# Two tiles' q and k turned into one bank ahead of its copies

## The chip, the cores and the metric

The kernel runs on one core of a Trainium2 chip. The metric is the device time of one execution in microseconds. Before the change three runs took 1618.83, 1619.05 and 1622.59 us; their median is 1619.05 us. Less is better.

## The reference

One layer of a bidirectional encoder: a sequence of 1024 tokens, model width 1024, everything in float32. Two attention branches share one input projection, and a gated feed-forward block follows. What concerns the change is the normalised q and k of each attention head:

```python
proj = h @ w_in[l]
qa, ka, va, qb, kb, vb, gates = jnp.split(proj, split_at, axis=-1)

qa = rms_norm(qa.reshape(b, s, NA_HEADS, HEAD_DIM), g_qa[l])
ka = rms_norm(ka.reshape(b, s, NA_HEADS, HEAD_DIM), g_ka[l])
o_a = neighbourhood_attention(qa, ka, va, rpb[l])

qb = partial_rotary(rms_norm(qb.reshape(b, s, DIL_HEADS, HEAD_DIM), g_qb[l]), pos)
kb = partial_rotary(rms_norm(kb.reshape(b, s, DIL_HEADS, HEAD_DIM), g_kb[l]), pos)
for g, (win, dil) in enumerate(DIL_CONFIGS):
    o_g, lse_g = dilated_window_attention(qb[:, :, sl], kb[:, :, sl], vb[:, :, sl], win, dil)
```

There are 12 dilated heads in three groups (windows 128, 512 and 2048 with dilations 1, 4 and 16) and 8 neighbourhood heads, each of 64 columns. The scores multiply q with k over these 64 columns, so both are needed with the columns on the partitions, that is, transposed.

## The kernel before, in words

The heads are worked on in pairs, called units: two units for each of the three dilated groups (kinds 0, 1 and 2, units 0 to 5) and four for neighbourhood attention (kind 3, units 6 to 9). A unit has 8 tiles of 128 tokens. One counter n runs over the tiles, u, t = divmod(n, 8), and iteration n projects tile t of unit u: 8 chunks (proj_chunk, L288) of three matmuls of 384 columns (high part times high part, high times low, low times high) into a bank of tag "d", four chunks in the first half of the iteration, four in the second. After that proj_post (L305) reads the bank: ScalarE squares and copies q and k (sq, qn), VectorE sums and scales (L314 to L316), GpSimd does the rotary part of kinds 0 to 2 (L323 to L326). The tile qn then holds the finished q (columns 0 to 127) and k (128 to 255), tokens on the partitions.

qk_turn (L347) turns a tile: two TensorE transposes of 128 x 128 (L352) into PSUM, and four copies out of it. ScalarE writes the high part of q with its gain (L370) and the high part of k (L371); VectorE writes the remainders of both (L372, L373). The parts go to U.qk, in an order of tokens that depends on the unit's kind. Each of these four copies has 128 columns.

Up to n = 57 the attention work stands in the middle of every odd iteration, between the two halves of the projection: scores of a cluster of items (L511), its maxima on VectorE (L521) and exponentials on ScalarE (L523), the product with v of the cluster from two odd iterations before (L556), the turns of two tiles (those of iterations n - 3 and n - 2), and the transposes of the previous cluster's P (L536). Such a pair of turns shares one PSUM bank of 512 columns: the first tile takes columns 0 to 255, the second 256 to 511. Unit 0 has four pairs (n = 8, 9, 11 and 13), the later units 24. From n = 58 on each iteration turns one tile alone, in a bank of its own; there are 24 of these.

A bank (L68) is a PSUM tile of one tag out of "d", "s", "v" and "t", two buffers each. Dependencies are kept for the tile: a write into a bank waits for the reads of it that stand earlier in the program. TensorE's order is the order of the program. In this part of the kernel the order on ScalarE, VectorE, GpSimd and the DMA queue is set by a scheduler that plays a timeline, with a priority on some functions. The weights of the next unit are loaded during a unit and split into a high part (ScalarE, L108) and a low part (GpSimd or VectorE, L109) at its end, six of the eight in t = 7, into ten buffers of each kind.

Beside this VectorE sums a vector-matrix product from loads of wa (L282), with a row sum on TensorE every eight steps (L259), and prepares pieces for later stages (L719 to L729).

Of the kernel before, what the change touches and what calls it, by code (L numbers as in the profile page):

```python
# [42 lines left out]
def hybrid_layer(ctx: ExitStack, tc: tile.TileContext, x, colp, wada1, wada2, bada2, wqkv, wg, wpa, wpb,  # L43
                 wo, w1, w2, hgain, ropeg, rope, rbias, bmask, g2r, out):
    nc = tc.nc
# [22 lines left out]
    def bank(tag):  # L68
        return ps.tile([128, 512], F32, tag=tag, name="ps_" + tag)
# [9 lines left out]
    ident = const.tile([128, 128], F32, name="ident")  # L79
# [16 lines left out]
    def fview(ap):  # L96
        return ap.bitcast(F32)
# [6 lines left out]
    def wsplit(r, eng=None):  # L104
        n = r.shape[1]
        hi = wp.tile([128, 512], F32R, tag="hi", bufs=NHL, name="whi")
        lo = wp.tile([128, 512], F32R, tag="lo", bufs=NHL, name="wlo")
        nc.scalar.activation(hi[:, :n], r, AF.Copy)  # L108
        (eng or nc.gpsimd).tensor_sub(lo[:, :n], r, fview(hi[:, :n]))  # L109
        return hi, lo  # L110
# [56 lines left out]
    def unit_load(u, k):  # L167
        return wload(wqkv[u, :, k, :], 384)
# [119 lines left out]
    def proj_chunk(U, t, k):  # L288
        if k == 0:
            U.pd[t] = bank("d" if U.u else "t")  # L290
        pd = U.pd[t]
        for i, (a, b) in enumerate(PASS):
            nc.tensor.matmul(pd[:, :384], tok(a, k, t), U.w[k][b][:, :384],  # L293
                             start=(k == 0 and i == 0), stop=(k == KT - 1 and i == 2))

    def urgent(off):
        def deco(f):
            def g(*a):
                with tc.high_priority(off):
                    return f(*a)  # L300
            return g
        return deco
# [41 lines left out]
                    nc.sync.dma_start(U.v[:, j, :], vv[j])  # L344

    @urgent(QT)
    def qk_turn(U, t, tag="v", pt=None):  # L347
        qf = U.qn[t].rearrange("p h d -> p (h d)")
        if pt is None:
            pt = bank(tag)  # L350
        for i in range(2):
            nc.tensor.transpose(pt[:, i * 128:(i + 1) * 128], qf[:, i * 128:(i + 1) * 128], ident)  # L352
        g = hg[:, 0:1] if U.kind == 3 else hg[:, 2:3]
        ops = []
        for i in range(2):
            hi, lo = U.qk[2 * i], U.qk[2 * i + 1]
            src = pt[:, i * 128:(i + 1) * 128]
            if U.kind == 0:
                hi, lo = hi[:, t * 128:(t + 1) * 128], lo[:, t * 128:(t + 1) * 128]
            elif U.kind < 3:  # L360
                n = 4 * U.kind
                c = slice(t * 128 // n, (t + 1) * 128 // n)
                hi, lo = (z.rearrange("p (r i) -> p r i", r=n)[:, :, c] for z in (hi, lo))
                src = src.rearrange("p (i r) -> p r i", r=n)
            else:
                hi, lo = (z.rearrange("p (w r) -> p r w", r=16)[:, 2 * t:2 * t + 2] for z in (hi, lo))
                src = src.rearrange("p (r w) -> p r w", r=2)
            ops.append((hi, lo, src))
        (qh, ql, qs), (kh, kl, ks) = ops
        nc.scalar.activation(qh, qs, AF.Identity, scale=g)  # L370
        nc.scalar.activation(kh, ks, AF.Copy)  # L371
        nc.vector.scalar_tensor_tensor(ql, qs, g, fview(qh), op0=ALU.mult, op1=ALU.subtract)  # L372
        nc.vector.tensor_sub(kl, ks, fview(kh))  # L373

    def new_unit(u, w):
        U = Unit()
        U.kind, U.pair = UNITS[u]
        U.u = u
        U.w = w
        U.pd, U.qn = {}, {}  # L380
        qk = ap_.tile([128, 4, S], F32R, tag="qk", bufs=2, name="qk")
        U.qk = [qk[:, i, :] for i in range(4)]
        U.v = big("v", [128, 8, 128])
        if U.kind < 3:
            U.tab = rtab[0] if rtab else None
            U.st = ap_.tile([128, 9, 4], F32, tag="st", bufs=2, name="st")
        else:
            U.bias = []
            for h in range(2):
                b = big("rb", [128, 768])  # L390
                nc.sync.dma_start(b, rbias[U.pair * 2 + h])
                U.bias.append(b)
        return U
# [352 lines left out]
    U = new_unit(0, w0)  # L746
# [143 lines left out]
    for n in range(6, 92):  # L890
        u, t = divmod(n, 8)
        if u < 10:
            if t == 0:
                units.append(new_unit(u, [nextw[u, k] for k in range(KT)]))
            U = units[u]
            chunks = [lambda k=k, U=U, t=t: proj_chunk(U, t, k) for k in range(KT)]
        elif n - 80 < NPRE:
            chunks = gate_pre(n - 80)
        else:
            chunks = []  # L900
        if u + 1 < 10:
            for k in ([0, 1, 2, 3, 4, 5, 6, 7] if n == 6 else [t] if u else []):
                raws[u + 1, k] = unit_load(u + 1, k)
            if t == 6:
                for k in range(2):
                    nextw[u + 1, k] = wsplit(raws[u + 1, k])
        if t == 2 and 1 <= u <= 10:
            for slot, I in unit_items(units[u - 1]):
                if I.U.kind < 3:
                    waiting.append(I)  # L910
                else:
                    ready.setdefault(8 * u + 2 + slot, []).append(I)
        if n == 8 * 7 + 5:
            combine_stats()
        ci = n - (8 * 7 + 7)
        if 0 <= ci < 12:
            combine_prep(ci)
        if n >= PAIRED:
            done, prev, cur = prev, cur, ready.pop(n, [])
        elif n % 2:  # L920
            done, prev, cur = prev, cur, []
            if waiting:
                cur = [Cluster()]
                while waiting and cur[0].keys + waiting[0].nkb * 128 <= 512:
                    cur[0].add(waiting.pop(0))
        else:
            done = []

        def chunk():
            if chunks:  # L930
                chunks.pop(0)()
                k = 8 - len(chunks)
                if t == 7 and u + 1 < 10 and k < 8 and k >= 2:
                    nextw[u + 1, k] = wsplit(raws[u + 1, k], nc.vector if k % 2 else None)

        turns = [(units[0], tt) for tt in {8: (0, 1), 9: (2, 3), 11: (4, 5), 13: (6, 7)}.get(n, ())]
        if PAIRED <= n <= 81 or 9 < n < PAIRED and n % 2:
            turns += [(units[m // 8], m % 8) for m in ((n - 2,) if n >= PAIRED else (n - 3, n - 2)) if m >= 8]
        chunk()
        chunk()  # L940
        chunk()
        chunk()
        if n < 10:
            while chunks:
                chunk()
        if n >= PAIRED or n % 2 or n < 10:
            for I in cur:
                if I.__class__ is Cluster:
                    cl_scores(I)
                    cl_qk(I)  # L950
                else:
                    at_scores(I)
                    at_qk(I, 0)
                    at_qk(I, 1)
            for I in done:
                (cl_pv if I.__class__ is Cluster else at_pv)(I)
            for j, q in enumerate(turns):
                if j % 2 == 0:
                    pq = bank("s" if n < 10 else "v")
                qk_turn(*q, "v", pq[:, 256 * (j % 2):256 * (j % 2) + 256])  # L960
            for I in prev:
                if I.__class__ is Cluster:
                    cl_turn(I)
                else:
                    at_turn(I, 0)
                    at_turn(I, 1)
        chunk()
        chunk()
        chunk()
        chunk()  # L970
        if n >= 8 and (t != 7 or u > 8) and ada_state["i"] < 65:
            ada_step()
        if 2 <= u < 6 and t < 5:
            if t in (2, 4):
                t_piece(2 * (u - 2) + t // 2 - 1, 2)
            if t in (0, 2):
                t_piece(2 * (u - 2) + t // 2, 0)
            if t in (1, 3):
                t_piece(2 * (u - 2) + t // 2, 1)
        if n in (85, 88):  # L980
            w1_combos((n - 85) // 3, EARLY[(n - 85) // 3])
        if 1 <= ci < 13:
            combine_step(ci - 1)
        while chunks:
            chunk()
        if u < 10:
            proj_post(U, t)
# [642 lines left out]
```

## Time and profile before

| what | value |
|---|---|
| median of 3 runs | 1619.05 us |
| profiled execution | 1627.35 us |
| its span, first to last instruction | 1625.5 us |
| mean granted TensorE clock over the span | 0.971 |
| TensorE busy | 1538.7 us, 95% |
| VectorE busy | 1109.7 us, 68% |
| ScalarE busy | 670.8 us, 41% |
| GpSimd busy | 532.2 us, 33% |

The engines are called PE (TensorE's matmuls), PEld (its weight loads), DVE (VectorE), ACT (ScalarE), POOL (GpSimd) and SP (the queue of loads and stores). A row of a timeline gives start and duration in us, engine, line, and what is written from what; in brackets the idle time before it on its engine and what ended that time. A list of waits gives the waiting line, the line waited for, the total in us, the number of times and the longest. Where a wait has several conditions, the row names what came last by the profile, which need not be the condition that mattered. The windows view cuts the span into stretches and gives busy times and the clock that TensorE was granted, 1.00 being full speed.

### The profile page before, as it was taken

Reading aid. Unit: us, or ns where it says so; the run is one execution under the profiler, and the core shown is the slowest. Engines: PE = TensorE matmul, PEld = TensorE weight load, DVE = VectorE, ACT = ScalarE, POOL = GpSimd, SP = SyncE. Lnnn points to the kernel's source line nnn. Section 1 sums busy time; section 2 is a strip of 40 time slices with the busy share of each in tenths; the row PEclk is TensorE's granted clock in tenths of the full one; section 3 lists DMA queues with packets and bytes.
Section 4 is the critical chain, followed back from the end, with each engine's and each line's share of the span. In section 5 each row is a group of like instructions: output and inputs, shape, how many; then the busy total and the mean of one; then the engine's idle time right before and its main releaser. Section 6 shows DMA issues by size and latency. Waiting matters only on the chain. (4 is left out here: it accounts for less than half of the span.)

```text
span 1625.5 us, 24441 instructions
## 1 busy us (share of the span) xinstructions
PE 1538.7 (95%) x8156; PEld 1301.9 (80%) x8156; DVE 1109.7 (68%) x2374; ACT 670.8 (41%) x1694; POOL 532.2 (33%) x540
## 2 busy tenths in 40 slices
PE   9978788888889999999999999999999999999998
PEld 7877778777778878788887888888888888887887
DVE  6745565555568996446567449778877777589567
ACT  5535444444445445433454234433223333344442
POOL 0512122122011001300045221167767777302564
PEclk9989898998999999999999999999999999999999
DMA  9603353343243343565354523534543333699343
GB/s 367 220 9 111 120 161 95 114 155 95 69 153 103 113 149 91 179 194 222 101 160 137 186 82 102 178 119 145 179 143 104 104 104 112 204 365 338 109 151 101
DMA packets 154414, 241.66 MB, mean 149 GB/s; under 512 B 26656, under 2 KB 73376, under 8 KB 153520
## 3 DMA queue, kind: packets, MB, share of 16 engines
q1 hardware_dynamic: 153136, 235.90, 44.5%
q10 hardware_dynamic: 1152, 4.19, 0.7%
q8 instruction: 65, 1.06, 0.3%
q14 instruction: 61, 0.50, 0.1%
HBM read 179.89 MB, written 60.15 MB: 148 GB/s over the span
## 5 line engine op out<-in xcount | busy, mean ns | idle before, releaser
L109 POOL TENSOR_TENSOR wlo<-raw,whi 128x512 fp32r<-128x512 f32 (+2 forms) x133 | 174.3, 1320 | 501.7 <-ACT whi L108 316.8
L293 PE MATMUL ps_d<-whi,hT 128*128 128x384 f32 x1152 | 329.9, 359 | 0.0
L108 ACT ACTIVATE whi<-raw 128x512 fp32r<-128x512 f32 (+1 forms) x348 | 205.5, 600 | 291.8 <-PE ps_s L1466 36.1
L109 DVE TENSOR_TENSOR wlo<-raw,whi 128x512 fp32r<-128x512 f32 (+1 forms) x215 | 181.6, 857 | 80.4 <-ACT whi L108 76.5
L293 PEld LDWEIGHTS ps_d<-whi,hT 128*128 128x128 f32 x1152 | 227.3, 203 | 5.2 <-issue 2.6
L293 PE MATMUL ps_d<-wlo,hT 128*128 128x384 f32 x576 | 203.7, 354 | 0.4 <-POOL wlo L109 0.4
L293 PEld LDWEIGHTS ps_d<-wlo,hT 128*128 128x128 f32 x576 | 117.0, 203 | 0.7 <-POOL wlo L109 0.7
L352 PE MATMUL ps_v<-ident,qn 128*128 128x128 f32 x152 | 35.0, 317 | 66.9 <-DVE qk L373 53.6
L108 ACT ACTIVATE whi<-ws 128x512 fp32r<-128x512 f32 x65 | 40.9, 629 | 130.1 <-DVE ws L1313 76.3
L323 POOL TENSOR_TENSOR ra<-qn,rtab 128x64 f32<-128x64 f32 x48 | 16.3, 339 | 231.4 <-DVE qn L316 212.7
L1246 POOL TENSOR_TENSOR e<-e,c 128x512 f32<-128x512 f32 x44 | 68.5, 1557 | 63.9 <-DVE c L1376 39.7
L314 DVE TENSOR_REDUCE ss<-sq 128x4 f32<-128x256 f32 x80 | 33.3, 416 | 74.2 <-ACT sq L311 74.1
L352 PEld LDWEIGHTS ps_v<-ident,qn 128*128 128x128 f32 x152 | 16.3, 150 | 80.5 <-issue 42.3
L311 ACT ACTIVATE sq<-ps_d 128x256 f32<-128x256 f32 x74 | 28.2, 382 | 112.7 <-PE ps_d L293 109.7
L109 POOL TENSOR_TENSOR wlo<-m,whi 128x512 fp32r<-128x512 f32 x35 | 51.6, 1483 | 54.4 <-ACT whi L108 54.4
L523 ACT ACTIVATE P<-P,st 128x256 f32<-128x256 f32 (+2 forms) x100 | 45.3, 455 | 41.8 <-DVE st L521 41.8
L680 PE MATMUL ps_d<-hT,whi 128*128 128x512 f32 x192 | 60.6, 396 | 0.0
L1296 PE MATMUL ps_v<-h2T,whi 128*128 128x512 f32 x192 | 59.3, 390 | 0.0
L1296 PE MATMUL ps_s<-h2T,whi 128*128 128x512 f32 x192 | 59.2, 390 | 0.0
L459 ACT ACTIVATE P<-P,sx 128x384 f32<-128x384 f32 (+1 forms) x64 | 37.0, 579 | 50.5 <-DVE sx L458 50.5
L1244 ACT ACTIVATE e<-e 128x512 f32<-128x512 f32 x44 | 27.4, 630 | 72.5 <-DVE e L1379 47.2
L1296 PE MATMUL ps_d<-h2T,whi 128*128 128x512 f32 x184 | 56.9, 390 | 0.0
(445 smaller groups left out, 4057.2 us busy)
## 6 DMA issues: line engine op xcount, KB each, us to landing
raw<-in_w_dram SPq DMA_DIRECT2D x139, 256.0 KB
ga_d<-e SPq DMA_DIRECT2D x77, 256.0 KB
raw<-ga_d SPq DMA_DIRECT2D x77, 256.0 KB
wa<-in_wada_dram SPq DMA_DIRECT2D x32, 512.0 KB
raw<-in_wqkv_dram SPq DMA_DIRECT2D x80, 192.0 KB
m<-in_w_dram SPq DMA_DIRECT2D x44, 256.0 KB
raw<-in_wg_dram SPq DMA_DIRECT2D x42, 256.0 KB
xt<-in_x_dram SPq DMA_DIRECT2D x16, 512.0 KB
```

The lines of the kernel that those rows point to most:

```text
L108: nc.scalar.activation(hi[:, :n], r, AF.Copy)
L109: (eng or nc.gpsimd).tensor_sub(lo[:, :n], r, fview(hi[:, :n]))
L293: nc.tensor.matmul(pd[:, :384], tok(a, k, t), U.w[k][b][:, :384], start=(k == 0 and i == 0), stop=(k == KT - 1 and i == 2))
L311: nc.scalar.activation(sq, pd[:, :256], AF.Square)
L314: nc.vector.tensor_reduce(ss, sq.rearrange("p (h d) -> p h d", h=4), axis=mybir.AxisListType.X, op=ALU.add)
L352: nc.tensor.transpose(pt[:, i * 128:(i + 1) * 128], qf[:, i * 128:(i + 1) * 128], ident)
L459: nc.scalar.activation(P[:nq, :nk], P[:nq, :nk], AF.Exp, scale=-1.0, bias=nm, accum_out=sm)
L523: nc.scalar.activation(C.P[h][:nq, c], C.P[h][:nq, c], AF.Exp, scale=-1.0, bias=nm, accum_out=sm)
L680: nc.tensor.matmul(st["p"], gw[i, br][j][a][:, kk * 128:(kk + 1) * 128], hT[b][:, k, hs], start=(k == 0 and q == 0), stop=(k == 7 and q == 2))
L1244: nc.scalar.activation(sg, a, AF.Sigmoid)
L1246: nc.gpsimd.tensor_mul(sg, sg, up)
L1296: nc.tensor.matmul(pb, w[p][:, k * 128:(k + 1) * 128], b[q][:, k], start=(k == 0 and i == 0), stop=(k == 3 and i == 2))
```

## The change

The turn of two tiles becomes one function, qk_turns. It issues all four transposes into one bank, sorted q of the first tile, q of the second, k of the first, k of the second, and then copies out with four instructions of 256 columns (qk_parts) in place of eight of 128. The two tiles are neighbours, so their tokens lie side by side in each of the layouts. A single tile goes through the same functions with n = 1: as before, two transposes and four copies of 128 columns.

```diff
     @urgent(QT)
-    def qk_turn(U, t, tag="v", pt=None):
-        qf = U.qn[t].rearrange("p h d -> p (h d)")
-        if pt is None:
-            pt = bank(tag)
-        for i in range(2):
-            nc.tensor.transpose(pt[:, i * 128:(i + 1) * 128], qf[:, i * 128:(i + 1) * 128], ident)
+    def qk_turns(tiles, tag):
+
+        bk = bank(tag)
+        n = len(tiles)
+        for j, (U, t) in enumerate(tiles):
+            qf = U.qn[t].rearrange("p h d -> p (h d)")
+            for i in range(2):
+                c = (i * n + j) * 128
+                nc.tensor.transpose(bk[:, c:c + 128], qf[:, i * 128:(i + 1) * 128], ident)
+        qk_parts(*tiles[0], n, bk)
+
+    def qk_parts(U, t, n, bk):
+
         g = hg[:, 0:1] if U.kind == 3 else hg[:, 2:3]
         ops = []
         for i in range(2):
             hi, lo = U.qk[2 * i], U.qk[2 * i + 1]
-            src = pt[:, i * 128:(i + 1) * 128]
+            src = bk[:, i * n * 128:(i + 1) * n * 128]
             if U.kind == 0:
-                hi, lo = hi[:, t * 128:(t + 1) * 128], lo[:, t * 128:(t + 1) * 128]
+                hi, lo = (z[:, t * 128:(t + n) * 128] for z in (hi, lo))
             elif U.kind < 3:
-                n = 4 * U.kind
-                c = slice(t * 128 // n, (t + 1) * 128 // n)
-                hi, lo = (z.rearrange("p (r i) -> p r i", r=n)[:, :, c] for z in (hi, lo))
-                src = src.rearrange("p (i r) -> p r i", r=n)
+                m = 4 * U.kind
+                c = slice(t * 128 // m, (t + n) * 128 // m)
+                hi, lo = (z.rearrange("p (r i) -> p r i", r=m)[:, :, c] for z in (hi, lo))
+                src = src.rearrange("p (i r) -> p r i", r=m)
             else:
-                hi, lo = (z.rearrange("p (w r) -> p r w", r=16)[:, 2 * t:2 * t + 2] for z in (hi, lo))
-                src = src.rearrange("p (r w) -> p r w", r=2)
+                hi, lo = (z.rearrange("p (w r) -> p r w", r=16)[:, 2 * t:2 * t + 2 * n] for z in (hi, lo))
+                src = src.rearrange("p (r w) -> p r w", r=2 * n)
             ops.append((hi, lo, src))
         (qh, ql, qs), (kh, kl, ks) = ops
         nc.scalar.activation(qh, qs, AF.Identity, scale=g)
...
-            for j, q in enumerate(turns):
-                if j % 2 == 0:
-                    pq = bank("s" if n < 10 else "v")
-                qk_turn(*q, "v", pq[:, 256 * (j % 2):256 * (j % 2) + 256])
+            for j in range(0, len(turns), 2):
+                qk_turns(turns[j:j + 2], "s" if n < 10 else "v")
```

In the changed kernel the transposes stand in L355, the copies in L377 to L380, and the lines behind them are numbered 7 higher (5 higher from L964 on).

TensorE at the first pair, n = 8 (qn is the tile that is turned, ps_s the bank; brackets name what a row waits for), before and then after:

```order
L293 MATMUL ps_d<-whi,hT_391 128x384
L352 MATMUL ps_s<-ident,qn 128x128 [waits PE_49]
L352 MATMUL ps_s<-ident,qn 128x128
L352 MATMUL ps_s<-ident,qn 128x128 [waits DVE_49]
L352 MATMUL ps_s<-ident,qn 128x128
L293 MATMUL ps_d<-whi,hT_106 128x384
```

```order
L293 MATMUL ps_d<-whi,hT_391 128x384
L355 MATMUL ps_s<-ident,qn 128x128 [waits PE_49]
L355 MATMUL ps_s<-ident,qn 128x128 x3
L293 MATMUL ps_d<-whi,hT_106 128x384
L293 MATMUL ps_d<-wlo,hT_106 128x384
```

The wait for VectorE between the two tiles is gone; the number and place of the transposes are the same.

TensorE at the pair of n = 15 (tiles 12 and 13; the pair that the prediction shows in the timeline), before and then after:

```order
L556 MATMUL ps_v<-PT,v 64x128 x2
L352 MATMUL ps_v<-ident,qn 128x128 [waits Pool_49]
L352 MATMUL ps_v<-ident,qn 128x128
L352 MATMUL ps_v<-ident,qn 128x128 [waits DVE_49,Pool_49]
L352 MATMUL ps_v<-ident,qn 128x128
L536 MATMUL ps_t<-ident,P 128x128 x8
```

```order
L563 MATMUL ps_v<-PT,v 64x128 x4
L355 MATMUL ps_v<-ident,qn 128x128 [waits DVE_49,Pool_49]
L355 MATMUL ps_v<-ident,qn 128x128
L355 MATMUL ps_v<-ident,qn 128x128 [waits DVE_49,Pool_49]
L355 MATMUL ps_v<-ident,qn 128x128
L543 MATMUL ps_t<-ident,P 128x128 x8
```

The rows stand in the same order. The second tile's wait still names both engines, which both write qn; the first tile's now names VectorE too, and the rows before it have fewer waits.

ScalarE at the same pair, before and then after:

```order
L523 ACTIVATE P,st<-P,st 128x256 [waits DVE_49] x2
L370 ACTIVATE qk<-ps_v,hg 128x128 [waits PE_49]
L371 ACTIVATE qk<-ps_v 128x128
L523 ACTIVATE P,st<-P,st 128x256 [waits DVE_49] x2
L370 ACTIVATE qk<-ps_v,hg 128x128 [waits DVE_49,PE_49]
L371 ACTIVATE qk<-ps_v 128x128
L545 ACTIVATE PT<-ps_t 128x512 [waits PE_49]
```

```order
L530 ACTIVATE P,st<-P,st 128x256 [waits DVE_49] x2
L377 ACTIVATE qk<-ps_v,hg 128x256 [waits PE_49]
L378 ACTIVATE qk<-ps_v 128x256
L530 ACTIVATE P,st<-P,st 128x256 [waits DVE_49] x2
L552 ACTIVATE PT<-ps_t 128x512 [waits PE_49]
```

The copies of both tiles now stand where the first tile's stood, in the middle of the exponentials; the second pair of copies is gone.

## The prediction

> **What bounds the kernel now.** I read the page first, then one stretch of the windows view, then TensorE's own waits in that stretch, then the timeline around one pair of turns. The page says where TensorE's time is not at full clock (forty slices of 40.6 us):
>
> ```profile
> span 1625.5 us, 24441 instructions
> ...
> PEclk9989898998999999999999999999999999999999
> ```
>
> The low digits stand in the first twelve slices, so in the projection stage. The windows view of that stage (n = 8 to 57, 73 to 474 us), of four short stretches inside it, and of the stretch just after it; columns: stretch, length, busy us of PE, PEld, DVE, ACT and POOL with instruction counts, granted clock, DMA share, GB/s:
>
> ```profile
> 73.00:474.00 401.00, 329.62 (x2088) 303.58 (x2087) 226.98 (x776) 179.66 (x645) 81.46 (x204) 0.89 0.35 108
> 127.00:131.00 4.00, 1.14 (x16) 0.72 (x14) 3.91 (x16) 2.15 (x9) 1.44 (x4) 0.85 0.73 207
> 131.00:134.00 3.00, 2.91 (x13) 2.94 (x14) 1.05 (x3) 1.47 (x5) 0.33 (x2) 0.50 0.61 238
> 134.00:137.00 3.00, 3.00 (x12) 3.00 (x11) 0.74 (x2) 1.57 (x3) 1.03 (x2) 0.56 0.00 0
> 137.00:140.00 3.00, 3.00 (x19) 3.00 (x18) 1.70 (x6) 1.63 (x6) 2.00 (x2) 1.00 0.01 3
> 474.00:570.00 96.00, 93.50 (x671) 82.37 (x671) 85.09 (x287) 50.96 (x172) 7.75 (x7) 1.00 0.39 119
> ```
>
> TensorE idles 401.00 - 329.62 = 71.4 us of the stage and has a mean clock of 0.89; after it, where turns come singly, it is 97% busy at 1.00. DVE is at 57% in the stage and ACT at 45%: neither bounds it. TensorE's waits in 73 to 474 us, the whole list (total us, times, longest):
>
> ```profile
> PE ps_v L352 <- DVE qk L373: 53.6, 21, 6.2
> PE ps_v L352 <- POOL rb L325: 8.8, 3, 3.0
> PE ps_v L352 <- POOL qn L326: 4.6, 2, 2.6
> PE ps_s L352 <- DVE qk L373: 4.5, 2, 2.6
> ```
>
> They sum to 71.5 us in 28 waits, as many as there are pairs of turns (4 of unit 0, 24 of later units), and all stand before one line, the transposes of qk_turn. So the idle time of the stage is this one wait. The timeline of one pair (start, us, engine, line) shows what it is:
>
> ```profile
> 127.70 0.44 PE L352 MATMUL ps_v<-ident,qn 128*128 128x128 f32 x2
> ...
> 129.85 0.34 ACT L370 ACTIVATE qk<-ps_v,hg 128x128 fp32r<-128x128 f32 x1
> 130.11 0.26 ACT L371 ACTIVATE qk<-ps_v 128x128 fp32r<-128x128 f32 x1
> 130.39 0.35 DVE L372 SCALAR_TENSOR_TENSOR qk<-ps_v,hg,qk 128x128 fp32r<-128x128 f32 x1
> 130.66 0.28 DVE L373 TENSOR_TENSOR qk<-ps_v,qk 128x128 fp32r<-128x128 f32 x1
> 131.09 0.66 PE L352 MATMUL ps_v<-ident,qn 128*128 128x128 f32 x2 [2.95 <-POOL rb L325]
> 131.54 1.91 PE L536 MATMUL ps_t<-ident,P 128*128 128x128 f32 x8
> ...
> 133.58 0.52 PE L293 MATMUL ps_d<-wlo,hT 128*128 128x384 f32 x1
> 134.54 0.52 PE L293 MATMUL ps_d<-wlo,hT 128*128 128x384 f32 x1
> ...
> 137.07 0.33 PE L293 MATMUL ps_d<-wlo,hT 128*128 128x384 f32 x1
> 137.59 0.33 PE L293 MATMUL ps_d<-wlo,hT 128*128 128x384 f32 x1
> ```
>
> Tile 12's q and k are transposed at 127.70. Tile 13's go into the same bank and stand still until the last of tile 12's four copies has left it (L373 ends at 130.94). The row names POOL only because a rotary step happened to end then too; the copy is what the bank waits for. ACT and DVE get to these copies late, because the exponentials and maxima of the cluster stand ahead of them. After the wait the clock is half: chunks of three matmuls follow each other at 134.54 - 133.58 = 0.96 us, against 137.59 - 137.07 = 0.52 us once it is back, and the windows show 0.50 and 0.56 there.
>
> **The change, part by part.**
>
> *1. The wait goes.* All four transposes stand ahead of any copy, and the order shows that the second tile's lose their DVE wait at n = 8 and keep elsewhere only waits for their own inputs. 28 waits, 71.4 us. Those inputs must be there earlier now. The latest case of the stage:
>
> ```profile
> 175.89 0.44 PE L352 MATMUL ps_v<-ident,qn 128*128 128x128 f32 x2
> 176.00 0.38 POOL L326 TENSOR_TENSOR qn<-ra,rb 128x64 f32<-128x64 f32 x1
> ```
>
> Tile 19's last rotary step ends at 176.38, while its transposes could now start at 175.89 + 0.44 = 176.33; by the same rows of the other 27 pairs (L326, or L316 where a unit has no rotary) the input was there before the first tile's transposes began, in two of them by under 0.35 us. Between the end of a projection and its turn lie an even iteration, half an odd one and the attention matmuls, all PE work and no pair wait, so this margin shrinks only where the clock was low there.
>
> *2. The half clock goes with it.* Two estimates. The first: 0.11 of 401 us is 44 us of lost clock. Part of it fell into the waits themselves, where it costs nothing (0.15 x 4 = 0.6 us in 127 to 131); at 0.4 a pair that is 11 us, and 33 us stay. The second compares periods:
>
> ```profile
> 147.43 0.41 PE L352 MATMUL ps_v<-ident,qn 128*128 128x128 f32 x2 [1.83 <-DVE qk L373]
> ...
> 199.76 0.41 PE L352 MATMUL ps_v<-ident,qn 128*128 128x128 f32 x2 [2.86 <-POOL rb L325]
> 200.00 1.04 PE L536 MATMUL ps_t<-ident,P 128*128 128x128 f32 x8
> ...
> 211.25 0.44 PE L352 MATMUL ps_v<-ident,qn 128*128 128x128 f32 x2
> ...
> 470.39 0.44 PE L352 MATMUL ps_v<-ident,qn 128*128 128x128 f32 x2 [1.52 <-DVE qk L373]
> ```
>
> From second turn to second turn 20 periods take (470.39 - 147.43) / 20 = 16.15 us. The stretch 199.76 to 211.25, 11.49 us, ran at full clock (its eight transposes took 1.04 us, against 1.91 at 131.54). A mean period without its wait (71.4 / 28 = 2.55) and the first turn (0.44) is 13.16, 1.67 above it. Some of it is work that only a few periods have, the one-row sums:
>
> ```profile
> L259 PE MATMUL ps_t<-acc,ones 128*1 128x512 f32 x10 | 5.1, 591 | 0.0
> ```
>
> Over 24 periods that is 0.2, so 1.47 a pair, 41 us over 28. I take 35, nearer to the first estimate, which counts the whole stage and not one stretch as the yardstick.
>
> *3. Fewer, wider copies.* Per pair eight copies become four of 256 columns. Price, from the forms view (mean ns of one):
>
> ```profile
> L370 ACT ACTIVATE qk<-ps_v,hg 128x128 fp32r<-128x128 f32 x52 | 19.5, 375 | 34.1 <-PE ps_v L352 34.1
> L372 DVE SCALAR_TENSOR_TENSOR qk<-ps_v,hg,qk 128x128 fp32r<-128x128 f32 x52 | 18.8, 362 | 35.1 <-ACT qk L371 34.8
> ...
> L311 ACT ACTIVATE sq<-ps_d 128x256 f32<-128x256 f32 x50 | 19.1, 382 | 98.2 <-PE ps_d L293 98.1
> L564 DVE COPY stg<-ps_v 128x256 f32<-128x256 f32 x15 | 6.2, 416 | 0.0
> ```
>
> A 256-column read of PSUM takes 0.38 on ACT and 0.42 on DVE, against 0.36 and 0.36 for 128 columns with the gain. At 0.4 to 0.5 each, a pair costs ACT 0.9 instead of 1.2 us, DVE 0.9 instead of 1.3. Neither bounds the stage, so I count nothing; at worst, were they as dear as two narrow ones, still nothing changes. The copies as a whole start about 0.5 us later for the first tile; their readers are the scores two iterations on.
>
> *4. What becomes late next.* PE now reaches everything behind the pair some 3.8 us sooner. The tightest partner is the weight split at a unit's start, where hi and lo of the next unit may only be written as PE frees the buffers:
>
> ```profile
> 202.20 3.30 POOL L109 TENSOR_TENSOR wlo<-raw,whi 128x384 fp32r<-128x384 f32 x3 [2.17 <-ACT whi L108]
> ...
> 206.28 0.33 PE L293 MATMUL ps_d<-wlo,hT 128*128 128x384 f32 x1
> ```
>
> The last lo was ready at 205.50, 0.78 us ahead of its matmul. With up to 2.5 us less time for ACT ahead of it, I put 1.5 us of new wait on each of the six unit starts in the stage: 9 us (0 to 18). For second tiles that come late, projection banks not yet read and DVE held up by late loads: 0.3 a pair, 8 us (0, since no such wait exists today, to 1.3 a pair, the excess clock loss of today taken as a yardstick: 36). And where new waits come, the clock may fall again: four of the 28 periods at 1.7 us, 7 us (0 to 20).
>
> **Sum.** 71.4 + 35 - (9 + 8 + 7) = 82 us. The profiled execution took 1627.35 us (1625.5 of span and 1.9 around it), 8.3 above the median of the three runs; from the median 1619.05 the forecast is **1537 us**. With nothing given back 1513; with the three upper bounds, 74 us, together 1587, which needs all three at once.
>
> The Trainium skill, "TensorE: Matmul & The Clock Gate", Part 4 (PE-mode transpose), says that full clock does not engage for transposes, since they do not count as PE work in the same way. By that, the half clock would belong to the transposes and not to the wait, and the change, which puts twelve in a row, would keep it. The trace speaks rather against it: 474 to 570 us has turns and transposes of P in every iteration, at 1.00. It is the second rival.
>
> **The rivals.**
>
> *The engines off the path become the path* (0.13). DVE and ACT are in-order and partly wait for loads whose latency does not shrink. For it: 6.2 us, the longest wait, came from such a hold-up. Against it: 227 us of DVE work in the 295 us left is 77%, and 474 to 570 us runs at 89% with TensorE 97% busy. If the stage could use DVE only to 65%, it would last 349 us: a gain of 52, **1567 us**.
>
> *The half clock stays* (0.07). Only the waits go, and what PE gives back goes on: 71.4 - 24 = 47 us, **1572 us**.
>
> *Slower* (0.02): the second tile is not ready, PE stands before it with the whole iteration behind, and both tiles' copies, now one piece, start only then; ACT stands at them with exponentials behind it. It decides once the new wait and its half clock exceed the 106 us / 28 = 3.8 us per pair taken away. At 5 us, 28 x 1.2 = 34 us more: **1653 us**. Against it: the rows of tile 19, 0.05 us late in the worst pair.
>
> *Nothing happens* (0.02): the second tile still waits for some copy. Against it stands the lost wait in the order; 1619 us.
>
> **How the numbers follow.** The forecast has 0.76, with 1513 to 1565 as its own range. Taking in half of the first two rivals, the range is 1512 to 1570. Faster by over 0.3% (about what a measurement of this kernel can tell from no change) are the forecast and the first two rivals, 0.96; same 0.02; slower 0.02.
>
> **What would show it.** Step 1: no wait of the transposes for DVE's qk, four in a row within 0.9 us, TensorE's idle time in the stage near 20 us instead of 71. Step 2: clock of the stage 0.97 or more, eight transposes of P always near 1.04 us. Step 3: 112 copies fewer, of 256 columns, at 0.4 to 0.5 us. Step 4: new waits of L293 for lo parts at unit starts. The forecast is wrong if the stage's PE idle time stays above 45 us under another name, or if the clock stays near 0.89 without waits.

## The result, and the profile after

| what | before | after |
|---|---|---|
| median of 4 runs each | 1618.94 us | 1523.96 us |
| lowest and highest | 1618.48, 1622.59 | 1523.19, 1527.91 |
| profiled execution | 1627.35 us | 1524.07 us |
| its span | 1625.5 us | 1522.3 us |
| mean granted TensorE clock | 0.971 | 0.998 |

The ratio is 0.9414, 95% interval 0.9392 to 0.9435: 95.0 us faster. The forecast was 1537, and the range of 1512 to 1570 holds the result. The two profiled executions lie further apart, 103.3 us, because that of before was 8.4 us above the median of its four runs. The kernel before varies more than the changed one: its 35 runs in this study lie between 1616.64 and 1628.36 us, the 12 of the changed kernel between 1522.30 and 1527.91.

The page of the changed kernel, its head and the line of the clock (forty slices of 38 us):

```profile
span 1522.3 us, 24290 instructions
...
PE 1499.0 (98%) x8156; PEld 1267.7 (83%) x8156; DVE 1101.9 (72%) x2318; ACT 657.4 (43%) x1638; POOL 538.4 (35%) x540
...
PEclk9999999999999999999999999999999999999999
```

The low digits of the first twelve slices are gone. TensorE's busy time fell from 1538.7 to 1499.0 us with the same number of matmuls: this part of the gain, 39.7 us, is not time that TensorE spent waiting.

The stage itself has become shorter, so its windows have other borders. It goes from 73 us to 364 us, where it went to 474, and the second row is the stretch behind it. Columns as in the prediction:

```profile
73.00:364.00 291.00, 288.00 (x2084) 267.51 (x2083) 217.44 (x719) 166.18 (x589) 88.71 (x204) 1.00 0.47 145
364.00:460.00 96.00, 91.00 (x634) 80.06 (x634) 81.10 (x275) 48.49 (x165) 5.74 (x5) 0.98 0.40 122
```

The stage takes 291.0 us instead of 401.0. Of these 110.0 us, idle time of TensorE gives (401.00 - 329.62) - (291.00 - 288.00) = 68.4, and busy time 329.62 - 288.00 = 41.6, with the clock at 1.00 instead of 0.89. The second row shows something that was not there before: in the stretch behind the stage TensorE is busy 91.0 of 96 us at 0.98, where it was 93.5 at 1.00.

TensorE's waits in 73 to 364 us, the whole list (total us, times, longest):

```profile
PE ps_d L293 <- DVE wlo L109: 1.9, 1, 1.9
PE ps_v L355 <- DVE qn L316: 0.5, 1, 0.5
PE ps_d L293 <- ACT vs L331: 0.3, 1, 0.3
PE ps_v L355 <- POOL qn L326: 0.2, 1, 0.2
```

No wait for a copy of qk is left. The two waits of L355 are second tiles whose input came a little late, 0.2 and 0.5 us. The timeline of one pair (TensorE, then the first copy):

```profile
119.08 0.66 PE L355 MATMUL ps_v<-ident,qn 128*128 128x128 f32 x4
119.58 1.04 PE L543 MATMUL ps_t<-ident,P 128*128 128x128 f32 x8
...
120.80 0.45 ACT L377 ACTIVATE qk<-ps_v,hg 128x256 fp32r<-128x256 f32 x1
```

Four transposes in 0.66 us, the eight of P behind them at 1.04, and the projection goes on while the copies are still to come: the first starts 1.7 us after the transposes began. ACT and DVE are no earlier than before: over the 28 pairs the first copy starts 1.9 us after a pair's first transpose, where it was 1.4 us. Nothing on TensorE waits for them any more.

### The profile page after: what moved, and what is told of

It reads as the page before. It is cut to its first block, busy times and chain, and to the rows that moved or that the text cites. A ratio compares the mean times of both kernels' runs of the same rounds, so it can differ in the third digit from the quotient of the medians.

```text
span 1522.3 us, 24290 instructions
## 1 busy us (share of the span) xinstructions
PE 1499.0 (98%) x8156; PEld 1267.7 (83%) x8156; DVE 1101.9 (72%) x2318; ACT 657.4 (43%) x1638; POOL 538.4 (35%) x540
## 5 line engine op out<-in xcount | busy, mean ns | idle before, releaser
L109 POOL TENSOR_TENSOR wlo<-raw,whi 128x512 fp32r<-128x512 f32 (+2 forms) x133 | 173.0, 1314 | 469.4 <-ACT whi L108 417.6
L293 PE MATMUL ps_d<-whi,hT 128*128 128x384 f32 x1152 | 311.7, 342 | 0.3 <-ACT vs L331 0.3
L293 PEld LDWEIGHTS ps_d<-whi,hT 128*128 128x128 f32 x1152 | 210.4, 189 | 5.8 <-ACT vs L331 4.1
L293 PE MATMUL ps_d<-wlo,hT 128*128 128x384 f32 x576 | 193.9, 337 | 2.2 <-DVE wlo L109 1.9
L293 PEld LDWEIGHTS ps_d<-wlo,hT 128*128 128x128 f32 x576 | 109.0, 189 | 3.0 <-DVE wlo L109 2.2
L1251 POOL TENSOR_TENSOR e<-e,c 128x512 f32<-128x512 f32 x44 | 68.6, 1560 | 64.3 <-DVE c L1381 40.1
L282 DVE SCALAR_TENSOR_TENSOR acc<-wa,cact,acc 128x512 f32<-128x512 f32 x56 | 42.0, 749 | 20.6 <-DMA wa<-in_wada_dram 20.4
L109 DVE TENSOR_TENSOR wlo<-ws,whi 128x512 fp32r<-128x512 f32 x45 | 50.5, 1123 | 8.2 <-ACT whi L108 8.2
L119 ACT ACTIVATE ry<-ss,eps 128x4 f32<-128x4 f32 (+1 forms) x88 | 26.3, 299 | 67.4 <-DVE ss L314 65.2
L1250 DVE TENSOR_TENSOR e<-e 128x512 f32<-128x512 f32 x44 | 42.6, 975 | 17.3 <-ACT e L1249 17.1
```

What stands on the lines that cost most here:

```text
L282: nc.vector.scalar_tensor_tensor(ada_acc[c], wa, cact[:, kk:kk + 1], ada_acc[c], op0=ALU.mult, op1=ALU.add)
L1250: nc.vector.tensor_mul(sg, sg, a)
L1251: nc.gpsimd.tensor_mul(sg, sg, up)
```

## The experiments

The main theory after the result has two terms: the 71.4 us of waiting were TensorE's own order standing behind a copy, and the half clock, some 40 us, follows from TensorE being idle. The rivals: the wide copies carry part of the gain (the change does two things at once); the half clock belongs to the transposes and not to the idle time; and the engines off the path now limit what is gained. Short diffs below are against the changed kernel unless the text says before.

**The changed kernel again**, as the yardstick on the chip on which three of the kernels below ran (narrow copies, the read, pairs to the end).

> The changed kernel once more, as the yardstick for the others on the same chip: 1524 us, within 0.3%.

Measured: 1525.5 us, ratio 0.9402 (0.9381 to 0.9423), clock 0.998. The result repeats within 2 us.

**Narrow copies, transposes still ahead.** The four transposes stay together, the copies are eight of 128 columns again:

```diff
-        qk_parts(*tiles[0], n, bk)
+        for j, (U, t) in enumerate(tiles):
+            qk_parts(U, t, n, j, bk)
...
-            src = bk[:, i * n * 128:(i + 1) * n * 128]
+            src = bk[:, (i * n + j) * 128:(i * n + j + 1) * 128]
```

> All four transposes stand ahead of the copies, but the copies are eight of 128 columns again. Theory (the gain is the wait between the tiles and the half clock behind it): same as the changed kernel, 1524 to 1528 us. Rival (the wide copies, 0.4 us less of ACT and DVE work per pair, carry a part): the lost share comes back, 28 x 0.8 = 22 us at most, 1535 to 1546 us, with new PE waits at unit starts.

Measured: 1522.93 us, ratio 0.9392 (0.937 to 0.9413), which cannot be told from the changed kernel. Copies in the forms view of the stage, first two of this kernel (x50: one a tile), then all four of the changed one (x26: one a pair; the two pairs in bank ps_s stand in other rows); columns: count, busy us, mean ns, idle before and what ended it:

```profile
L378 ACT ACTIVATE qk<-ps_v,hg 128x128 fp32r<-128x128 f32 x50 | 18.6, 372 | 7.7 <-DVE qk L381 5.3 <-PE ps_v L355 2.2
L380 DVE SCALAR_TENSOR_TENSOR qk<-ps_v,hg,qk 128x128 fp32r<-128x128 f32 x50 | 17.8, 356 | 8.3 <-ACT qk L379 8.1
```

```profile
L377 ACT ACTIVATE qk<-ps_v,hg 128x256 fp32r<-128x256 f32 x26 | 12.8, 492 | 3.4 <-PE ps_v L355 3.4
L379 DVE SCALAR_TENSOR_TENSOR qk<-ps_v,hg,qk 128x256 fp32r<-128x256 f32 x26 | 13.3, 511 | 4.4 <-ACT qk L378 4.4
L380 DVE TENSOR_TENSOR qk<-ps_v,qk 128x256 fp32r<-128x256 f32 x26 | 11.6, 445 | 0.0
L378 ACT ACTIVATE qk<-ps_v 128x256 fp32r<-128x256 f32 x26 | 10.6, 409 | 0.0
```

A copy of q with its gain costs 492 ns for 256 columns against 372 for 128 on ACT, and its remainder 511 against 356 on DVE, so a pair saves 2 x 372 - 492 = 252 ns and 2 x 356 - 511 = 201 ns on these two. It is saved where no one waits, and does not show in the time. The gain belongs to the order of the transposes; the copies have no share in it that these intervals, some 3.5 us to either side each, would show.

**A read between the two tiles.** The changed kernel, with one tiny read of the bank by ACT after the first tile's transposes. The read is work added; the output is unchanged.

```diff
         for j, (U, t) in enumerate(tiles):
...
+            if n == 2 and j == 0:
+                tiny = ap_.tile([128, 1], F32, tag="tiny", bufs=2, name="tiny")
+                nc.scalar.activation(tiny, bk[:, 0:1], AF.Copy)
```

> The changed kernel with a read of one column of the bank by ACT between the two tiles, so that the second tile's transposes wait again, while the wide copies stay. Theory: the wait comes back less the time of the copies themselves (about 1 us of the 2.55), so 1.5 us x 28 = 42 us, and a part of the half clock with it, 10 to 35 us: 1575 to 1600 us. Rival (wide copies carry the gain, the wait is hidden): below 1540 us. Rival (waits under 2 us cost no clock): 1566 us at a clock of 0.99.

Measured: 1570.42 us, ratio 0.9678 (0.9655 to 0.9701). One column read by ACT puts about half of the wait back. TensorE's waits in 73 to 413.2 us, where the stage of this kernel ends (without a last one of 0.4 us in L293), and the windows row of that stretch:

```profile
PE ps_v L355 <- issue: 28.8, 18, 3.3
PE ps_v L355 <- ACT tiny L358: 4.2, 6, 2.3
PE ps_v L355 <- POOL rb L325: 2.2, 1, 2.2
PE ps_v L355 <- POOL qn L326: 2.0, 1, 2.0
PE ps_s L355 <- ACT tiny L358: 1.5, 2, 0.8
```

```profile
73.00:413.20 340.20, 301.49 (x2091) 275.81 (x2090) 218.99 (x720) 173.79 (x617) 82.18 (x205) 0.97 0.41 126
```

The five rows of L355 make 38.7 us. Most of them are put down to "issue" or to GpSimd; the one thing that this kernel adds is the tiny read, so the names say little and the line that waits says all. Reads of one column do not take 38 us. What is paid is the time that ACT needs to get to them, behind the exponentials: TensorE pays the other engine's lateness, not its work. The clock fell to 0.97 only. PE busy is 301.49 - 288.00 = 13.5 us above the changed kernel's stage, of which 8.5 us are lost clock behind waits (below). The wait came near the 42 us expected, the lost clock did not reach the 10 to 35 us, and the time lies 5 us under the forecast of 1575 to 1600, nearest to the rival by which waits under 2 us cost no clock (1566 us at 0.99). Not by its reason either: 5 of this kernel's 23 waits halve the clock (below), the shortest of 1.58 us.

**Transposes alone, many of them.** The transposes of a pair are issued ten times, or seven times, over (extra work, same output):

```diff
-        for j, (U, t) in enumerate(tiles):
+        for j, (U, t) in [*enumerate(tiles)] * (10 if n == 2 else 1):
```

> The changed kernel with each pair's four transposes issued ten times over, so that 40 of them and 8 of P follow each other, 5.3 us without an ordinary matmul and without an idle moment (before: about 4.5 us of wait and transposes). 36 more at 0.11 us, 28 times: 112 us. Theory (the half clock follows idle time): 1636 us, clock of the stage 0.99. Rival (transposes do not count as work for the clock, so a long row of them halves it as a wait does): half clock behind each of them, 1.3 us or more each and the last transposes slower, 1680 to 1710 us, clock of the stage 0.93 or less.

> The same with seven times over: 36 transposes in a row with those of P, 4.0 us. Theory (idle time alone): 24 x 0.11 x 28 = 75 us, 1599 us at 0.99. Rival (transposes do not count): 4.0 us without counted work is nearly what the pairs of before had, so a half clock behind most of them: 1620 to 1640 us at about 0.95.

Measured: 1630.12 us (ratio 1.005, 1.0032 to 1.0067) and 1595.37 us (0.9828, 0.9776 to 0.988; two runs alone, 7.7 us apart). The timeline of one pair and the windows row of the stage, both of the tenfold kernel:

```profile
131.60 4.58 PE L355 MATMUL ps_v<-ident,qn 128*128 128x128 f32 x40
136.02 1.04 PE L543 MATMUL ps_t<-ident,P 128*128 128x128 f32 x8
...
137.07 0.34 PE L293 MATMUL ps_d<-wlo,hT 128*128 128x384 f32 x1
...
137.60 0.35 PE L293 MATMUL ps_d<-wlo,hT 128*128 128x384 f32 x1
```

```profile
73.00:470.00 397.00, 394.23 (x3073) 374.53 (x3072) 219.38 (x716) 171.55 (x583) 82.97 (x205) 1.00 0.36 108
```

48 transposes in a row fill TensorE for 137.06 - 131.60 = 5.5 us. The clock of the stage is 1.00, the eight of P take the 1.04 us of full clock, and the chunks follow each other at 137.60 - 137.07 = 0.53 us at once. The stage as a whole is nearly as long as before (397 against 401 us) with a clock of 1.00 instead of 0.89. So transposes do not halve the clock here, and the rival falls. The Trainium skill, "TensorE: Matmul & The Clock Gate", Part 4 (PE-mode transpose), says that the gate does not go to full for them; this row shows them at full clock and leaving it at full clock. The two kernels also give the price of one: (1630.12 - 1523.96) / (28 x 36) = 0.105 us, and (1595.37 - 1523.96) / (28 x 24) = 0.106 us, each one in full on the path. (The changed kernel's 1523.96 us is from another chip; its repeats gave 1525.5 and 1524.43.)

**Before, with work between the two tiles.** Two experiments leave the bank shared and the copies narrow, and only put other TensorE work in front of the waiting transposes. The first moves the eight transposes of P there (the diffs are against the kernel before; the second piece keeps them from being issued twice):

```diff
+                elif j == len(turns) - 1 and n >= 10:
+                    for I in prev:
+                        cl_turn(I)
+                    prev_done = n
...
-            for I in prev:
+            for I in prev if prev_done != n else []:
```

> The kernel before, with the eight transposes of the previous cluster's P moved between the two tiles' turns, so that 1 us of the wait is filled with transposes. Waits shorter by about 1 us in some 24 pairs. If the half clock follows idle time, it becomes rare, as idle times of 1.5 us were nearly free of it in the run with the one-column read: 1619 - 24 - 28 = 1567 us. If it follows the time without ordinary matmuls, which shrinks by the same 1 us to about 3.5 us: also less, about half, 1580 us. If it came with every wait whatever its length: 1595 us.

Measured: 1597.23 us, ratio 0.9845 (0.981 to 0.988), a smaller gain than any theory had expected. It lies by the third number, 1595, but not for its reason: that one had the waits 24 us shorter and the clock loss unchanged, where the waits gave 11 us and the clock loss fell from 40.1 to 18.9 us (table below). TensorE's waits for the copies in 73 to 430 us:

```profile
PE ps_v L352 <- DVE qk L373: 53.7, 25, 4.2
PE ps_s L352 <- DVE qk L373: 4.8, 2, 2.6
```

58.5 us, and a last one of 1.5 behind 430 us make 60.0. It was 71.4: the 1.04 us of cover in 24 pairs should have taken 24 off, and took 11. The timeline of one of the worse pairs shows who gave it back:

```profile
284.54 0.44 PE L352 MATMUL ps_v<-ident,qn 128*128 128x128 f32 x2
...
284.81 1.04 PE L536 MATMUL ps_t<-ident,P 128*128 128x128 f32 x8
...
287.13 0.68 DVE L543 COPY PT<-ps_t 128x512 f32<-128x512 f32 x1
...
288.32 0.28 DVE L373 TENSOR_TENSOR qk<-ps_v,qk 128x128 fp32r<-128x128 f32 x1
...
288.75 0.66 PE L352 MATMUL ps_v<-ident,qn 128*128 128x128 f32 x2 [2.90 <-DVE qk L373]
```

The transposes of P now end sooner, so their copy (L543, 0.68 us) stands on DVE ahead of the copies that free the bank. It does so in 20 of the 24 pairs, with 0.42 us in one and 0.64 to 0.83 us in the others. The cover made its own delay.

The second puts the second half of the iteration's projection there, four chunks:

```diff
+                elif j == len(turns) - 1:
+                    for _ in range(4):
+                        chunk()
```

> The kernel before, with the second half of the projection (four chunks, 2.1 us of matmuls) moved between the two tiles' turns; the bank, the wait condition and the eight narrow copies stay. Theory (what costs is that PE stands in its own order behind the wait, not the sharing of the bank): 2.1 of the mean 2.55 us are filled, 1530 to 1545 us at a clock of 0.99. Rival (one bank shared by copies and transposes is itself slow, or the later second tile delays the scores): above 1570 us.

Measured: 1556.41 us, ratio 0.9581 (0.9546 to 0.9615), two thirds of the gain without touching the bank or the width of the copies. TensorE's waits in 73 to 400 us, the four longest rows:

```profile
PE ps_v L352 <- DVE qk L373: 16.7, 9, 3.8
PE ps_s L352 <- DVE qk L373: 4.6, 2, 2.6
PE ps_v L352 <- POOL rb L325: 2.5, 3, 0.9
PE ps_v L352 <- DVE ry L124: 1.5, 1, 1.5
```

The expectation was missed by 11 us: it had taken every wait as covered. At n = 8 and 9 there is no second half to move, at n = 11 and 13 only one of two waits lies behind it, and some waits are longer than the four chunks, 2.1 us. In the six iterations with t = 7 (n = 15 to 55) the moved chunks also bring weight splits to ACT, DVE and GpSimd, and every one of these keeps a wait, of 0.76 to 1.04 us and at n = 55 of 3.82. The mechanism is what was tested, and it holds: what costs is that TensorE's order has nothing else to do at this place.

**The stretch behind the stage.** In the changed kernel the stretch from the first single turn (n = 58) to the last (n = 81) takes 538.52 - 365.51 = 173.0 us; before it took 644.26 - 475.50 = 168.8. DVE has 81.1 busy of 96 us there (85.1 before), and it waits longer for loads of wa. Before and after, at the place where the stage ends (SP's issue of v and DVE's step that needs wa):

```profile
463.96 5.03 SPq L344 DMA_DIRECT2D v<-v_d  x8
470.56 0.36 SPq L276 DMA_DIRECT2D wa<-in_wada_dram  x1
476.59 0.75 DVE L282 SCALAR_TENSOR_TENSOR acc<-wa,cact,acc 128x512 f32<-128x512 f32 x1 [0.20 <-DMA wa<-in_wada_dram]
```

```profile
359.29 5.02 SPq L344 DMA_DIRECT2D v<-v_d  x8
365.87 0.37 SPq L276 DMA_DIRECT2D wa<-in_wada_dram  x1
371.93 0.75 DVE L282 SCALAR_TENSOR_TENSOR acc<-wa,cact,acc 128x512 f32<-128x512 f32 x1 [4.39 <-DMA wa<-in_wada_dram]
373.01 0.44 PE L477 MATMUL ps_t<-ident,P 128*128 128x128 f32 x2 [1.77 <-DVE P L469]
```

The load takes as long as before from its issue to the step that uses it (6.0 and 6.1 us). DVE gets there 4 us sooner and stands, and TensorE stands behind DVE for 1.8 us. Two kernels asked whether this can be got back. The first keeps pairs of turns until the end, so that DVE and ACT have fewer copies in that stretch:

```diff
-        if PAIRED <= n <= 81 or 9 < n < PAIRED and n % 2:
-            turns += [(units[m // 8], m % 8) for m in ((n - 2,) if n >= PAIRED else (n - 3, n - 2)) if m >= 8]
+        if 9 < n <= 81 and n % 2:
+            turns += [(units[m // 8], m % 8) for m in (n - 3, n - 2) if m >= 8]
```

> The changed kernel with pairs to the end: from n = 58 on two tiles are turned in every odd iteration in place of one in each. Theory (that stretch is held by DVE, 84 to 89% busy, where 12 pairs save 0.37 us each and 0.4 us of ACT): 2 to 6 us faster than the changed kernel, 1518 to 1522 us. Rival (the waits left there come from late loads, not from DVE work): no change, 1524 us.

Measured: 1525.15 us, ratio 0.9404 (0.9381 to 0.9426), no difference. The stretch and the row of DVE in it:

```profile
364.00:460.00 96.00, 89.92 (x629) 79.32 (x628) 78.91 (x259) 47.72 (x150) 5.70 (x5) 0.98 0.40 124
...
375.05 0.75 DVE L282 SCALAR_TENSOR_TENSOR acc<-wa,cact,acc 128x512 f32<-128x512 f32 x1 [5.27 <-DMA wa<-in_wada_dram]
```

DVE is busy 2.2 us less in this row, in part because this kernel issues the loads of v 2.5 us later there than the changed one, and it waits 5.27 us for the same load. What DVE stands for here is the load, and less work of its own did not shorten that.

The second takes the eight loads of v out of the way: they are issued two at a time in the four iterations that follow.

```diff
-            elif t == 7:
-                vv = vd.rearrange("(r j c) d -> j c r d", r=16, c=8)
-                for j in range(8):
-                    nc.sync.dma_start(U.v[:, j, :], vv[j])
...
+        if t < 4 and 7 <= u <= 10:
+            V = units[u - 1]
+            vv = v_d[V.u - 2].rearrange("(r j c) d -> j c r d", r=16, c=8)
+            for j in (2 * t, 2 * t + 1):
+                nc.sync.dma_start(V.v[:, j, :], vv[j])
```

> The changed kernel as the yardstick on the chip of the next run: 1524 us.

> The changed kernel with the eight loads of v of the neighbourhood units taken out of the end of a unit, where they hold the SP queue for 5 us, and issued two at a time in the first four iterations of the next unit. Theory (the 4.3 us lost again after n = 57 come from wa loads that stand behind these eight in the queue): the 4.4 us wait of DVE for wa at the start of n = 58 shrinks below 1 us, TensorE's waits behind it (2.6 us) go, 3 to 4 us faster than the changed kernel, 1520 to 1521 us. Rival (the load is late for its buffer or its own latency): wait unchanged, 1524 us.

Measured: 1522.2 us, ratio 0.9378 (0.9364 to 0.9393), beside 1524.43 us, 0.9383 (0.937 to 0.9395), of the changed kernel on the same chip: 2.2 us apart, and the intervals overlap. The place, in this kernel:

```profile
362.34 0.45 SPq L276 DMA_DIRECT2D wa<-in_wada_dram  x1
...
366.77 1.54 DVE L282 SCALAR_TENSOR_TENSOR acc<-wa,cact,acc 128x512 f32<-128x512 f32 x2 [3.53 <-DMA wa<-in_wada_dram]
```

wa is issued 3.5 us earlier than in the changed kernel's trace above, DVE still waits 3.53 us where under 1 was forecast, and its waits for wa sum to 21.6 us as against 22.3 in the changed kernel beside it. The stretch from the first to the last single turn is not shorter either, 173.5 us against 172.4. The queue ahead of the load was at most a part. What else holds it was not settled, and no kernel here is clearly better than the changed one.

**What the clock follows.** Five kernels are compared by their waits of TensorE in this stage of 0.5 us and more, the changed one by all. For each wait I took the granted clock over the 5 us behind its end, and counted 5 x (1 - clock) as lost. Two such windows of the kernel before, behind a wait of 2.95 and one of 1.83 us:

```profile
131.09:136.09 5.00, 5.00 (x19) 5.00 (x20) 1.36 (x4) 2.42 (x7) 1.32 (x2) 0.50 0.35 137
147.43:152.43 5.00, 5.00 (x28) 3.89 (x29) 2.13 (x5) 2.36 (x8) 0.00 (x0) 1.00 0.32 45
```

| kernel | waits, us (number) | lost to the clock, us | waits + clock - 3.0 | measured above the changed kernel's span, us |
|---|---|---|---|---|
| before | 71.4 (28) | 40.1 | 108.5 | 103.2 |
| transposes of P between | 60.0 (28) | 18.9 | 75.9 | 70.7 |
| tiny read between | 37.3 (23) | 8.5 | 42.8 | 42.5 |
| chunks between | 28.1 (19) | 11.0 | 36.1 | 33.4 |
| changed | 3.0 (4, all listed above) | none | 0 | 0 |

The two terms give the time of each kernel to within 0.3 to 5.3 us. They lie above it in every row, which is the side of the 6.7 us that the changed one loses behind its stage (below). The clock term is not a fixed share of the waits: 0.56 of them before, 0.23 with the tiny read. Among the 98 waits of the first four rows, a halved clock behind it (under 0.93 over the 5 us) came in

| length of the wait, us | halved |
|---|---|
| under 1.4 | 0 of 27 |
| 1.4 to 2.0 | 14 of 30 |
| 2.0 to 3.2 | 18 of 32 |
| over 3.2 | 9 of 9 |

The 10 halved ones under 1.75 have 1.58 to 1.67 us and all stand at n = 11 and 13. In the kernel before they are double waits, two of them 0.6 us apart; with the chunks between, where the second wait is gone, single ones of 1.64 and 1.67 us halve the clock too. Between 1.4 and 3.2 us length does not decide.

What decides for the most part is where the wait falls. In each of these four traces the granted clock is 1.00 or 0.50 and changes only on a raster of 3.413 us, whose start differs from trace to trace; the 37 half stretches of the stage are one or two such steps long, 3.41 or 6.83 us. Three steps of the kernel before, all at full clock, around a wait of 2.95 us (257.27 to 260.22) and one of 3.12 us (323.01 to 326.13):

```profile
256.11:259.52 3.41, 1.15 (x16) 0.73 (x14) 3.37 (x14) 1.54 (x7) 0.85 (x2) 1.00 0.70 196
320.96:324.38 3.42, 2.05 (x30) 1.51 (x26) 3.38 (x14) 1.43 (x6) 1.21 (x2) 1.00 0.46 128
324.38:327.79 3.41, 1.66 (x14) 1.70 (x15) 1.89 (x9) 2.54 (x11) 1.05 (x4) 1.00 0.46 142
```

The first wait leaves TensorE 1.15 us of work in one step, and the next step is at 0.50. The second, though longer, is divided over two steps that keep 2.05 and 1.66 us of work, and the clock stays at 1.00 behind both. All 371 steps at full clock in these four stages, by the share of the step in which TensorE was busy:

| busy share of a step | next step at half clock |
|---|---|
| under 0.42 | 26 of 26 |
| 0.42 to 0.61 | 10 of 35 |
| over 0.61 | 0 of 310 |

Idle time is meant, not time without ordinary matmuls: in the kernel with tenfold transposes 19 steps hold nearly nothing but transposes, and none is followed by a half one. What decides between 0.42 and 0.61 stays open.

## Why the prediction was right, and where its sums were off

**Step 1, the waits (71.4 us): right.** All of them went; 3.0 us came anew. Two second tiles were late, by 0.24 and 0.55 us; in the two repeats of the changed kernel the latest were late by 0.82 and 1.70 us. The margins of the kernel before did not tell which: tile 19, 0.05 us short there, was on time in the first profile and 0.2 us late at most, while the tiles that came late (9, 43 and 49) had 3.4 to 6.1 us in hand before the first tile's transposes. The tiny read shows the cause from the other side, and the chunks between the tiles show that it was TensorE's order and not the bank as such.

**Step 2, the half clock (35 us): right in kind, 41.6 in PE busy time (40.1 by the windows).** It was priced by two estimates, 33 and 41, and 35 was taken, near the lower, on the ground that this one counted the whole stage. The other, which set a mean period against a stretch at full clock, was the better one. The first went wrong where it took off 11 us as clock lost inside the waits, from one window of 4 us: the half stretches of the stage make 92.2 us, so 46.1 us are lost, and only 6.0 of them fall into waits. The tenfold transposes decide the cause that the prediction left at a chance of 0.07.

**Step 3, the copies (nothing): right.** They take 0.41 to 0.51 us, where 0.4 to 0.5 was forecast, and the kernel with narrow copies is as fast. (ACT's narrow copy, read as 0.36 us there, has 375 ns in the row shown.)

**Step 4, the give-back (24 us): the step that failed in size.** It was made of 9 us at unit starts, 8 us of late inputs and 7 us of clock. In the stage it measured 1.9 us at unit starts, 0.3 + 0.7 us of late inputs, and no clock. (The repeats have 3.1 and 4.3 us of waits there, and one of them a single step at half clock.) The start of a unit was priced at 1.5 us each for six; one of the six has a wait:

```profile
210.19 0.75 DVE L282 SCALAR_TENSOR_TENSOR acc<-wa,cact,acc 128x512 f32<-128x512 f32 x1 [2.58 <-DMA wa<-in_wada_dram]
...
212.87 0.44 PE L293 MATMUL ps_d<-wlo,hT 128*128 128x384 f32 x1 [1.87 <-DVE wlo L109]
```

There the low part was late because DVE had stood 2.58 us for wa. In the other five the splits kept up, although the margin seen before was only 0.78 us in the unit that was looked at. The prediction took the shorter time ahead of the splits as a loss at every unit, from one unit's rows.

What it did not have is a loss outside the stage: 173.0 - 168.8 = 4.2 us in n = 58 to 81, and 2.5 us behind (the stretch from the last single turn to the end has 983.8 us instead of 981.2). The second is less sure: the repeats of the changed kernel have 982.7 and 984.0 us there. The first is there in both, 173.3 and 172.4 us, and it goes with how early the stage ends: the kernels with a wait put back or left, which reach n = 58 at 405 to 443 us, take 167.7 to 168.7 us for it. It also goes with DVE's longer waits for wa (20.4 us in all, 16.5 before), as the first rival said ("wait for loads whose latency does not shrink"), at 4 us instead of 30; half of it is idle time, half busy time of TensorE, with one step at half clock (375.58 to 379.00 us, 1.7 us lost) behind the wait of 1.77 us shown above. That the late loads cause all of it was not shown. For the second stretch, the longest row in the list of TensorE's waits behind the last single turn is a weight split, in the changed kernel and before:

```profile
PE ps_d L1471 <- DVE wlo L109: 2.6, 3, 2.1
```

```profile
PE ps_d L1466 <- DVE wlo L109: 1.0, 3, 0.5
```

Why it is later there was not followed up.

**The sum.** 71.4 + 35 - 24 = 82 was forecast; 71.4 + 41.6 - 3.0 - 6.7 = 103.3 came, on the profiled executions. The clock was 7 us too small and the give-back 14 us too large. Taken off the median, 1619.05 - 103.3 would be 1516; the measured 1524 is 8 us above, since the profiled execution of before had 8.3 us more to lose than a usual run. The forecast took the gain from that execution and the starting point from the median, and so carried an error of 8 us that, by luck, hid part of the other: 13 us are missing in the forecast, 21 us in its sum.

**The rivals.** The off-path engines cost 4 us, not 30: DVE ran at 217.44 / 291.00 = 75% in the stage, well over the 65% at which that rival would have put it. The half clock went with the waits. A second tile that is late, the slower case, occurred twice, at 0.24 and 0.55 us, and in a repeat once at 1.70, under the 3.8 us a pair at which it would decide. The wait did go, so "nothing" fell.

## What to carry to other kernels

When a list of waits names a copy out of a shared bank, look at what stands behind the waiting transposes in TensorE's order: here two instructions that took 0.44 us held up the whole engine for 2.5 us a pair, and the remedy was to issue every write into the bank ahead of its first read, not to make the copies cheaper. A stall of TensorE can cost more than its length; compare the granted clock behind each stall, and read the clock's share from busy time (the same matmuls, 41.6 us less). Work put in front of a wait covers it in full only if it brings no work of its own to the engines that are waited for: four chunks took 4.2% off, eight transposes with their copies 1.6%.

## What the runs showed of the hardware

- The granted clock of TensorE was 1.00 or 0.50 and changed on a raster of 3.413 us. A step in which TensorE was busy for under 0.42 was followed by one at half clock in 26 of 26 cases, from 0.42 to 0.61 in 10 of 35, above that in 0 of 310. By length alone, waits halved the clock from 1.58 us on, in 32 of 62 of 1.4 to 3.2 us, always above 3.2, never under 1.4. After the wait of 2.95 us at 128 to 131 us the half clock ran from 129.81 to 136.64, until 5.5 us after the wait. The Trainium skill, "TensorE: Matmul & The Clock Gate", Part 1 (What's actually happening), puts the fall to at least one idle window of about 3.4 us, and says that the window runs freely. The raster in these traces agrees with it; but the step need not be idle throughout, since 1.4 us of work in 3.41 us (0.42) did not hold the clock.
- fp32 transposes of 128 x 128 cost 0.105 us each in a row and hold the full clock, 48 of them one after the other.
- One 128 x 1 read by ACT between two pairs of transposes into the same bank cost 45 us over 28 pairs (1570.42 - 1525.5), although the later transposes write other columns: the kernel's dependencies are kept for the whole bank.
